# An own tile for the memory's transposed squares, and the other sequence's row squares transposed and summed in two steps

## The chip, the cores and the metric

The kernel runs on one core of a Trainium2 chip. The metric is the device time of one execution in microseconds (us), the median of several runs. Engines are named as the profile names them: PE (TensorE), DVE (VectorE), ACT (ScalarE), POOL (GpSimd) and SP (SyncE, which here only issues DMAs).

## The reference, cut to what matters

One encoder layer runs over two sequences of 512 tokens with 1024 channels each. In float32 it computes:

```
x = x + 0.5 * swiglu(rms_norm(x, ffn1_norm))                 # d_ff 2816
proj = rms_norm(x, mix_norm) @ w_in                          # q, k, v, memory q, k, v, gates
att  = attention(q, k, v)                                    # 8 heads of 64, 2 kv heads
mem  = sigmoid(o) * rms_norm_per_head(h_fwd + h_bwd)         # 4 memory heads of 128
x = x + (sigmoid(g_a) * (att @ w_up_att) + sigmoid(g_m) * (mem @ w_up_mlstm)) @ w_out
x = x + 0.5 * swiglu(rms_norm(x, ffn2_norm))
y = rms_norm(x, final_norm)
```

Two norms matter here. `rms_norm(x, ...)` needs, for each token, the sum of squares over 1024 channels. `rms_norm_per_head` needs, for each token and memory head, the sum of squares over 128 channels.

## The kernel before, in words

Activations lie with channels on the 128 partitions and the 512 tokens along the free axis. Every matrix product is made of three products of split values (high by high, high by low, low by high), each a 128x128 by 128x512 matmul on PE. So most tiles have a high part, which ACT writes by rounding, and a low part, which DVE writes by subtraction: both are in `split` (lines 725 to 728), the high part at L727 and the low part at L728.

The program has four stages: the first feed-forward network for both sequences, the mixing block of sequence 0 (generator `m0`), that of sequence 1 (`m1`), interleaved with the end of `m0`, and the second feed-forward network. A scheduler sets the order of instructions on each engine when the program is built, and it gives tiles their buffers out of pools in that order: a tile with the tag `f2` gets one of four buffers of 128x512 floats, a tile with the tag `R` one of two, and an instruction that writes a tile waits until the last reader of the tile that had the buffer before is done. Instructions wrapped in `pin` keep the order of the program text.

**Sums over partitions.** A sum of squares over channels is a sum over partitions. `block_sums` (L221 to L227) transposes the tile of squares in 32x32 blocks on DVE (L225) into a scratch tile with the tag `f2`, and reduces it to 128x16 on DVE (L226). `block_rstd` folds the four quarters with one small matmul on PE (L232) and takes the reciprocal root with twelve small DVE instructions (L235 to L241). `spread_rows` (L258) transposes the result back to 128x512.

**The other sequence's row squares in the attention.** While `m0` works through its eight attention heads (loop `for h in range(HA)`, `for b in range(4)`), it also makes the row norm of sequence 1, and `m1` makes the norm that sequence 0 needs for its second feed-forward network. These are passed in as `extra`: three functions `one`, `two` and `three` of `mid_parts` and `parts2`. They are called at b == 2 of heads 2, 3 and 4: `one` is `block_sums`, `two` is `block_rstd`, `three` is `spread_rows`. Beside them a head has DVE reduce each 128x512 score tile (L1115), take a reciprocal (L1118), scale some tiles (L1122), transpose probabilities in blocks (L1140), write low parts of probabilities (L728) and read the output bank (L1174); PE makes scores (L1112), values (L1159), transposes through the identity (L1128) and matmuls of the projection (L836) as filler in between.

**The memory heads of `m1`.** For each of four heads, `mem_head` makes the 512x512 weights, `mem_blocks` transposes them in 32x32 blocks on DVE (L1340), `mem_send` writes them to a DRAM buffer in eight DMAs on POOL's queue (L1348, `tbuf<-qt`), and `mem_out` reads them back in four pieces, each one DMA on POOL's queue (L1361, `f<-tbuf`) into a tile with the tag `f2`. Each piece is split (L727, L728), and PE multiplies it by the values: three matmuls a piece, `pso<-t,Vm` at L1374, two with the high part and one with the low. The DMAs of `mem_send` and `mem_out` and the L1374 matmuls are kept in program order among themselves; L850 matmuls (`mm<-att,w`, `mm<-xh,w`) fill PE in between. At the end of `mem_out` ACT copies and squares the sum (L1380, L1383), DVE multiplies the gate in (L1384), and then come `block_sums` into a tile `turned_` with the tag `f2`, `block_rstd`, `spread_rows` back into the same `turned_`, and its last reader at L1391. So `turned_` holds one of the four `f2` buffers from L225 to L1391, while the next head's pieces want four.

Among and after the last memory heads come eight units `mem_gate` (24 matmuls `mm<-xh,w` each, L850), most of them ahead of the fourth head's matmuls, and then the merge (L850, `pss<-mem,w`). In `m1` the first row blocks for the second network are prepared there: `prep2` loads a piece (L1808, `f<-x2buf`, tag `f2`, on SP), scales it (L723) and stores it (L1810, `xnbuf<-f`, on SP). SP also loads the weights (L293, `w<-wpark`).

Of the kernel before, what the change touches and what calls it, by code (L numbers as in the profile page):

```python
# [8 lines left out]
F32 = mybir.dt.float32  # L9
# [17 lines left out]
def encoder(ctx, tc, I, outs):  # L27
# [14 lines left out]
    def nm(s):  # L42
        n_id[0] += 1
        return f"{s}_{n_id[0]}"
# [15 lines left out]
    def T2(dtype=F32, tag="t2"):  # L60
        if tag in ("eb", "ac"):
            i = boxes[tag]
            boxes[tag] += 1
            return boxes["tile"][:, i % 4 + (4 if tag == "ac" else 0), :]
        if tag == "R":
            return spool.tile([P, S], dtype, tag="R", bufs=2, name=nm("R"))
        n = {"t2": 11, "f2": 4}[tag]
        return tpool.tile([P, S], dtype, tag=tag, bufs=n, name=nm(tag))
# [41 lines left out]
    def PO():  # L110
        return po_.tile([P, S], F32, tag="o", name=nm("pso"))
# [22 lines left out]
    def A(shape, dtype=F32, name="a"):  # L134
        return apool.tile(shape, dtype, tag="a", name=nm(name))
# [82 lines left out]
        nc.gpsimd.tensor_copy(fold[:, 32:P].rearrange("p (a j) -> p a j", j=32),  # L218
                              part_.unsqueeze(1).to_broadcast([P, 3, 32]))

    def block_sums(t, q=None):  # L221

        row = spool.tile([P, 64], F32, tag="row", bufs=1, name=nm("row"))
        q = T2(F32, "f2") if q is None else q
        nc.vector.transpose(q, t)  # L225
        nc.vector.tensor_reduce(row[:, 0:16], q.rearrange("p (n j) -> p n j", j=32), axis=AX.X, op=ALU.add)  # L226
        return row  # L227

# [630 lines left out]
    def mix(s, xh, xl, early=None, extra=None, after=None):  # L859
# [9 lines left out]
        def F2(dtype=F32):  # L869
            return T2(dtype, "f2")  # L870
# [136 lines left out]
        def gate_tops(run, top):  # L1007
            p = PT()
            pin(nc.tensor.transpose(p[:, 0:32], run, ident[0:32, 0:32]))
            pin(nc.tensor.transpose(p[:, 32:64], top.to_broadcast([32, P]), ident[0:32, 0:32]))  # L1010
            V_.tensor_copy(st[:, 0:2], p[:, 0:64].rearrange("p (i d b h) -> p i d b h", i=2, d=2, b=4))
# [44 lines left out]
        def q_rope(pr):  # L1056
            return rope_steps(qraw[:, :, pr * P:(pr + 1) * P], rq[0][:, :, 2 * pr:2 * pr + 2], tabs[0])

        def q_turn(pr, keep):
            p = pair_turn(qraw[:, :, pr * P:(pr + 1) * P], keep, MM if pr else PT)  # L1060
            for h, own, other in ((2 * pr, lower, upper), (2 * pr + 1, upper, lower)):
                nc.scalar.activation(qT[own, h, :], p[own, :], AF.Copy)
                V_.tensor_tensor(qT[other, h, :], p[own, :], f(qT[own, h, :]), op=ALU.subtract)
# [44 lines left out]
        def score(h, b):  # L1108
            hk = h // 4
            p = PS()  # L1110
            for j in range(2):
                pin(nc.tensor.matmul(p, qT[:, h, b * P:(b + 1) * P], kv[:, hk * 2 + j, :],  # L1112
                                     start=(j == 0), stop=(j == 1)))
            c = small(3, "asm")
            V_.tensor_reduce(c[:, 0:1], p, axis=AX.X, op=ALU.max, negate=True)  # L1115
            e = T2()
            nc.scalar.activation(e, p, AF.Exp, bias=c[:, 0:1], accum_out=c[:, 1:2])
            V_.reciprocal(c[:, 2:3], c[:, 1:2])  # L1118
            if b % 2 and (s or h or b < 3) or not s and h:
                nc.scalar.activation(e, e, AF.Copy, scale=c[:, 2:3])  # L1120
            else:
                V_.tensor_scalar(e, e, c[:, 2:3], None, op0=ALU.mult)  # L1122
            return e
# [15 lines left out]
        def turn_early(t, b):  # L1139
            V_.transpose(turned[:, :, b, :], t[:, 0:2 * P].rearrange("p (n m) -> p n m", m=32))  # L1140
# [63 lines left out]
        for h in range(HA):  # L1204
            nxt = []
            for b in range(4):
                if h in (0, 2, 4) and b == 2:
                    q_turn(h // 2 + 1, pin)
                if (h, b) == (0, 1):
                    gate_tops(*tops)  # L1210
                if (h, b) in ((0, 3), (2, 3)):
                    rope = q_rope(h // 2 + 2)
                if h < 4:
                    next(rope, None)
                if h + 1 < HA:
                    nxt.append(score(h + 1, b))
                if b in (3, 0) and h + b // 3 < (HA - 1 if not s else HA):
                    if b == 3:
                        for i in range(2):
                            turn_early(nxt[i], i)  # L1220
                    else:
                        for i in range(2, 4):
                            turn_early(Ps[i], i)
                if b == 1 and (h < HA - 1 or not (not s)):
                    send(h)
                n0, n1_ = FILLER if b else SOON
                among(n0)
                pp = None
                if b > 1:
                    pp = h, b, turn_keys(Ps, b)  # L1230
                elif h:
                    pp = h - 1, b, fetch(h - 1, b)
                among(n1_)
                if last:
                    values(*last)
                last = pp
                if extra and b == 2 and h in (2, 3, 4):
                    extra[h - 2]()
            Ps = nxt or Ps
        for b in range(2):  # L1240
            pp = HA - 1, b, turn_keys(Ps, b) if not s else fetch(HA - 1, b)
# [46 lines left out]
            return up_unit(1, d, mem, done, (PS, PT)[d % 2])  # L1288

        mem = A([P, HM, 2, S], F32R, "mem")  # L1290

        def mem_head(h):
            qk = qks[h]
# [58 lines left out]
        def mem_out(h, Ts):  # L1352
            moved = isinstance(Ts, int)
            vm = Vm[0]
            po = PO()
            hs_ = slice(h * P, (h + 1) * P)
            turned = []
            for j in range(4 + 1):
                if j < 4 and moved:
                    p = F2()  # L1360
                    mark(nc.gpsimd.dma_start(p, tbuf[Ts][4 * j:4 * j + 4].rearrange("c r a x -> (c r) (a x)")), True)  # L1361
                elif j < 4:
                    p = PT()
                    for i in range(4):
                        nc.tensor.transpose(p[:, i * P:(i + 1) * P], Ts[i][0][:, j * P:(j + 1) * P], ident)
                if j < 4:
                    ph, pl = T2(F32R), T2(F32R)
                    split(p, ph, pl)
                    turned.append((j, ph, pl))
                if j >= 1:  # L1370
                    t, ph, pl = turned.pop(0)
                    with shifted(15):
                        for n, (a, b) in enumerate(((0, ph), (1, ph), (0, pl))):
                            mark(nc.tensor.matmul(po, vm[:, a, t, hs_], b, start=(t == 0 and n == 0),  # L1374
                                                  stop=(t == 3 and n == 2)), True)
            h2 = T2()
            og = ogs[h]
            if moved:
                rows_ = T2()
                nc.scalar.activation(rows_.rearrange("p (i a m) -> p i a m", i=4, a=4),  # L1380
                                     po.rearrange("p (a i m) -> p i a m", i=4, a=4), AF.Copy)
                po = rows_
            nc.scalar.activation(h2, po, AF.Square)  # L1383
            V_.scalar_tensor_tensor(og, og, 1.0, po, op0=ALU.add, op1=ALU.mult)  # L1384
            turned_ = F2()
            row = block_sums(h2, turned_)
            with shifted(60):
                rh = block_rstd(row, DM)
            with shifted(160):
                Rh = spread_rows(rh, turned_)  # L1390
                V_.scalar_tensor_tensor(og, og, hn[:, h:h + 1], Rh, op0=ALU.mult, op1=ALU.mult)  # L1391
                split(og, mem[:, h, 0, :], mem[:, h, 1, :])

        if s:
# [3 lines left out]
            q = mem_blocks(0, mem_head(0))  # L1398
            at = [mem_send(*q)]
            go(*mem_values(), *qk2)  # L1400
            q = mem_blocks(1, mem_head(1))
# [3 lines left out]
            q = mem_blocks(2, mem_head(2))  # L1405
# [3 lines left out]
            q = mem_blocks(3, mem_head(3))  # L1409
# [338 lines left out]
    accs = [None, None]  # L1748
# [21 lines left out]
    R = [None, None]  # L1770
# [14 lines left out]
    def mid_parts(s):  # L1785
        got = []

        def one():
            got.append(block_sums(accs[s]))

        def two():
            got.append(block_rstd(got[0], D, pin))

        def three():
            R[s] = spread_rows(got[1], T2(F32, "R"))
        return one, two, three

    m0 = mix(0, *nhl[0], None, mid_parts(1), prep1)
    for _ in range(3):
# [1 line left out]
    acc2 = [None, None]  # L1801
# [14 lines left out]
    def parts2(s):  # L1816
        got = []

        def one():
            got.append(block_sums(acc2[s]))  # L1820

        def two():
            got.append(block_rstd(got[0], D, pin))

        def three():
            R2[s] = spread_rows(got[1], T2(F32, "R"))
        return one, two, three

    R2 = [None, None]
    m1 = mix(1, *nhl[1], None, parts2(0), prep2)  # L1830
# [152 lines left out]
```

## Time and profile before

| | us |
|---|---|
| median of 3 runs (lowest to highest) | 2033.63 (2033.22 to 2034.94) |
| the profiled execution | 2034.22 |
| its span, first to last instruction | 2032.4 |
| PE busy in the span | 2016.1 |
| DVE busy | 1593.8 |
| ACT busy | 919.9 |
| POOL busy | 253.4 |
| waits of PE for others, all together | 9.0 |

The profile is of one execution. A row of its timeline gives the start in us from the span's start, how long the rows merged in it took, engine, line, operation, output and inputs (buffer numbers left out), the shape, the count, and in brackets how long the engine had been idle before and what ended that. "f<-tbuf" is an instruction that writes a tile f from a tile tbuf. The waits of PE above are the sum of the rows "PE ... <- ..." of the table of waits (2.5, 1.6, 1.3, 1.0, 0.7, 0.7, 0.5, 0.3, 0.2 and 0.2). The matmul's ends in the profile are modelled; the starts are the better measure of PE's pace.

### The profile page before, as it was taken

The numbers are of one execution on the slowest core, as the hardware profiler recorded it, in microseconds if no ns is written. First come the engines' busy times: TensorE is split into PE (matmuls) and PEld (weight loads), VectorE is DVE, ScalarE is ACT, GpSimd is POOL, SyncE is SP. The second block draws the span as 40 slices with busy tenths as digits, with TensorE's granted clock in tenths as the row PEclk, the third lists the DMA queues.
The fourth block names the chain that finished last, engine by engine and source line by source line (L and its number), as shares of the span: only waits on it lengthen the run. The fifth ranks groups of instructions, "written<-read, shape, count | busy, mean of one in ns | idle before, by whom it ended". The sixth has DMA issues, their size and how long they took to land.

```text
span 2032.4 us, 26876 instructions
## 1 busy us (share of the span) xinstructions
PE 2016.1 (99%) x9129; PEld 1662.1 (82%) x9129; DVE 1593.8 (78%) x2830; ACT 919.9 (45%) x1677; POOL 253.4 (12%) x313
## 2 busy tenths in 40 slices
PE   9999999999999999999999999999999999999998
PEld 7888888888888887888888877888888888888887
DVE  7989999996698787886567867367798988786797
ACT  7644444443224477663325754145444444442224
POOL 0233333301003000100120022011000000000001
PEclk9999999999999999999999999999999999999999
DMA  9778786899766765868556677767565655699753
GB/s 312 232 234 266 237 276 229 276 346 363 270 218 225 266 195 184 282 212 293 194 188 209 195 246 259 252 204 242 159 208 169 227 166 180 204 334 348 270 199 120
DMA packets 329546, 482.11 MB, mean 237 GB/s; under 512 B 23016, under 2 KB 196160, under 8 KB 328128
## 3 DMA queue, kind: packets, MB, share of 16 engines
q1 hardware_dynamic: 316352, 439.27, 64.9%
q0 software_dynamic: 12896, 40.86, 5.8%
q8 instruction: 72, 1.18, 0.2%
q14 instruction: 66, 0.54, 0.1%
q10 hardware_dynamic: 160, 0.27, 0.0%
HBM read 308.70 MB, written 171.61 MB: 236 GB/s over the span
## 4 chain that ended last, share of the span: by engine, by line
PE 94%; DVE 2%; DMA 2%; ACT 1%; issue 0%; SPq 0%; DVEq 0%; ACTq 0%; POOLq 0%
PE mm L850 15%; PE pso L374 12%; PE pst L374 11%; PE mm L374 10%; PE mm L644 9%; PE pss L374 6%; PE mm L836 4%; PE pss L644 4%; PE pst L644 4%; PE mm L815 3%; PE pso L644 3%; PE pss L1112 1%; PE pso L1159 1%; PE pst L850 1%; PE pss L850 1%; PE pss L1302 1%
## 5 line engine op out<-in xcount | busy, mean ns | idle before, releaser
L374 PE MATMUL pst<-xc,w 128*128 128x512 f32 x1056 | 253.8, 389 | 1.0 <-ACT t L409 1.0
L374 PEld LDWEIGHTS pst<-xc,w 128*128 128x128 f32 x1056 | 198.2, 188 | 42.5 <-ACT t L409 1.4
L374 PE MATMUL mm<-xc,w 128*128 128x512 f32 x972 | 229.7, 390 | 0.3 <-ACT f L382 0.3
L374 PEld LDWEIGHTS mm<-xc,w 128*128 128x128 f32 x972 | 181.9, 188 | 38.6 <-ACT f L382 0.8
L644 PE MATMUL mm<-rt,w 128*128 128x512 f32 x765 | 178.7, 389 | 0.0
L850 PE MATMUL mm<-xh,w 128*128 128x512 f32 x560 | 176.3, 392 | 0.0
L644 PEld LDWEIGHTS mm<-rt,w 128*128 128x128 f32 x765 | 143.5, 188 | 29.7
L332 ACT ACTIVATE w<-t 128x512 fp32r<-128x512 f32 x176 | 107.5, 628 | 132.2 <-issue 63.1
L333 DVE TENSOR_TENSOR w<-t,w 128x512 fp32r<-128x512 f32 x176 | 120.8, 704 | 30.6 <-ACT w L332 28.9
L374 PE MATMUL pso<-xc,f 128*128 128x512 f32 x528 | 127.2, 390 | 0.1
L374 PE MATMUL pss<-xc,w 128*128 128x512 f32 x528 | 126.8, 389 | 0.0
L374 PE MATMUL pso<-xc,w 128*128 128x512 f32 x528 | 126.8, 389 | 0.0
L850 PEld LDWEIGHTS mm<-xh,w 128*128 128x128 f32 x560 | 105.2, 188 | 22.0
L374 PEld LDWEIGHTS pso<-xc,f 128*128 128x128 f32 x528 | 98.9, 188 | 21.5 <-DVE t L413 1.0
L374 PEld LDWEIGHTS pss<-xc,w 128*128 128x128 f32 x528 | 99.1, 188 | 20.6
L374 PEld LDWEIGHTS pso<-xc,w 128*128 128x128 f32 x528 | 99.1, 188 | 20.6
L836 PE MATMUL mm<-xh,w 128*128 128x512 f32 x336 | 110.4, 395 | 0.0
L850 PE MATMUL mm<-xl,w 128*128 128x512 f32 x280 | 109.7, 392 | 0.0
L727 ACT ACTIVATE w<-wr 128x512 fp32r<-128x512 f32 x72 | 45.1, 632 | 138.4 <-PE pso L644 70.6
L727 ACT ACTIVATE w<-t 128x512 fp32r<-128x512 f32 x82 | 51.8, 632 | 107.4 <-PE pst L644 62.4
L644 PE MATMUL pss<-rt,w 128*128 128x512 f32 x396 | 93.7, 389 | 0.0
L644 PE MATMUL pst<-rt,w 128*128 128x512 f32 x396 | 93.7, 389 | 0.0
(461 smaller groups left out, 4169.6 us busy)
## 6 DMA issues: line engine op xcount, KB each, us to landing
rt<-rbuf SPq DMA_DIRECT2D x154, 512.0 KB, 5.7
w<-wpark SPq DMA_DIRECT2D x112, 512.0 KB, 5.0
wpark<-w SPq DMA_DIRECT2D x64, 512.0 KB, 3.9
wr<-in_ffn_w_gate_dram SPq DMA_DIRECT2D x62, 512.0 KB, 5.5
wr<-in_ffn_w_up_dram SPq DMA_DIRECT2D x44, 512.0 KB, 4.7
rbuf<-f SPq DMA_DIRECT2D x86, 256.0 KB, 4.5
rbuf<-R SPq DMA_DIRECT2D x82, 256.0 KB, 4.7
rbuf<-tab SPq DMA_DIRECT2D x74, 256.0 KB, 4.1
```

The source lines that it names most:

```text
L332: pin(nc.scalar.activation(t[:, 0], src, AF.Copy))
L333: pin(V_.tensor_tensor(t[:, 1], src, f(t[:, 0]), op=ALU.subtract))
L374: nc.tensor.matmul(p, a[:, k, :], xt[:, b, k, :], start=(first and k == 0 and i == 0), stop=(k == HK_ - 1 and i == 2), skip_group_check=True)
L644: nc.tensor.matmul(p, u[:, a, d * P:(d + 1) * P], r[:, b, ts], start=(first and q == 0 and k == 0), stop=(q == len(us) - 1 and k == 2), sk ...
L727: nc.scalar.activation(hi, src, AF.Copy)
L815: mark(nc.tensor.matmul(p[b][:, :N], a[:, k, bs], w_[:, kl, :], start=(k == 0 and i == 0), stop=(k == KD - 1 and i == 2)), (kl, b, i) == ( ...
L836: pin(nc.tensor.matmul(p[0], a[:, k, :], b, start=(k == 0 and i == 0), stop=(k == n - 1 and i == 2)))
L850: mark(nc.tensor.matmul(p, a[:, k, :], b, start=(k == 0 and i == 0), stop=last), last)
L1112: pin(nc.tensor.matmul(p, qT[:, h, b * P:(b + 1) * P], kv[:, hk * 2 + j, :], start=(j == 0), stop=(j == 1)))
L1159: pin(nc.tensor.matmul(pos[h], Vst[:, kb, h // 4, :], w, start=(kb == KBS[0] and i == 0), stop=(kb == KBS[3] and i == 1)))
L1302: nc.tensor.matmul(p, qk[a][:, isl], qk[b], start=(n == 0), stop=(n == 2))
```

## The change

Three edits. The memory of `m1` gets one tile `own` with the tag `R`, made once, and all four heads use it as `turned_` in place of a new `f2` tile each. `block_sums` can stop after the transposition (`later=True`), and the new `block_adds` does the reduction. `one` becomes two functions, `one` and `one_`, and the schedule calls them at (h, b) = (2, 1) and (2, 2); `two` and `three` stay at (3, 2) and (4, 2).

```
-    def block_sums(t, q=None):
+    def block_sums(t, q=None, later=False):
         row = spool.tile([P, 64], F32, tag="row", bufs=1, name=nm("row"))
         q = T2(F32, "f2") if q is None else q
         nc.vector.transpose(q, t)
+        if later:
+            return row, q
+        return block_adds(row, q)
+
+    def block_adds(row, q):
         nc.vector.tensor_reduce(row[:, 0:16], q.rearrange("p (n j) -> p n j", j=32), axis=AX.X, op=ALU.add)
         return row
...
-                if extra and b == 2 and h in (2, 3, 4):
-                    extra[h - 2]()
+                if extra and (h, b) in ((2, 1), (2, 2), (3, 2), (4, 2)):
+                    extra[h - 2 + (h > 2 or b == 2)]()
...
         mem = A([P, HM, 2, S], F32R, "mem")
+        own = [T2(F32, "R")] if s else []
...
-            turned_ = F2()
+            turned_ = own[0] if own else F2()
             row = block_sums(h2, turned_)
...
         def one():
-            got.append(block_sums(accs[s]))
+            got.append(block_sums(accs[s], later=True))
+
+        def one_():
+            got[0] = block_adds(*got[0])
...
-        return one, two, three
+        return one, one_, two, three
```

`parts2` changes as `mid_parts` does, with `acc2` for `accs`. No instruction is added or taken away: PE, DVE, ACT, POOL and SP have as many as before. Buffers and the order are what differ. In the order of the changed program lines from L226 on have moved: L226 is L232 there, L232 is L238, L293 is L299, L728 is L734, L850 is L856, L1115 is L1121, L1118 is L1124, L1122 is L1128, L1140 is L1146, L1174 is L1180, L1374 is L1381, L1808 is L1818 and L1810 is L1820.

**PE, third memory head of `m1`.** These are the matmuls of its last two pieces (`pso`) among those of the attention's projection (`att`) and of the first `mem_gate` (`xh`, `xl`). Each piece has a high tile (x2) and a low one. Before:

```order
L1374 MATMUL pso_11385<-t_1457_11403,Vm_10719 128x512 x2
L850 MATMUL mm_11460<-att_9414,w_11354 128x512 x2
L1374 MATMUL pso_11385<-t_1458_11404,Vm_10719 128x512
L850 MATMUL mm_11477<-att_9414,w_11354 128x512 x3
L1374 MATMUL pso_11385<-t_1460_11412,Vm_10719 128x512 x2
L850 MATMUL mm_11477<-att_9414,w_11354 128x512 x3
L1374 MATMUL pso_11385<-t_1461_11413,Vm_10719 128x512
L850 MATMUL mm_11477<-att_9414,w_11354 128x512 x6
```

and in the changed program, up to the fold matmul of this head:

```order
L1381 MATMUL pso_11384<-t_1456_11402,Vm_10720 128x512 x2
L856 MATMUL mm_11458<-att_9414,w_11353 128x512 x2
L1381 MATMUL pso_11384<-t_1457_11403,Vm_10720 128x512
L1381 MATMUL pso_11384<-t_1459_11411,Vm_10720 128x512 x2
L1381 MATMUL pso_11384<-t_1460_11412,Vm_10720 128x512
L856 MATMUL mm_11475<-att_9414,w_11353 128x512 x12
L856 MATMUL mm_11492<-xh_8455,w_11455 128x512
L856 MATMUL mm_11492<-xl_8456,w_11455 128x512
L856 MATMUL mm_11492<-xh_8455,w_11455 128x512
L238 MATMUL pst_11429<-row_11426,fold 128x16
```

The last piece's three matmuls stand right behind the third piece's, ahead of the twelve that stood partly before them, and the fold matmul follows 15 matmuls after them (it was 15 before too, six of `att` and nine of the gate). POOL's order has not moved. What has is the buffer of the last piece: before, it takes over that of the first piece of the same head; now that of the last piece of the head before.

**DVE, attention of `m1`, head 2.** `R_9062` is the tile of squares. Before, the transposition and the sum stand among the work of b == 2:

```order
L1063 TENSOR_TENSOR qT_8643<-mm_9810,qT_8643 64x512
L728 TENSOR_TENSOR t_1169_9844<-pst_9838,t_1168_9843 128x512
L1174 TENSOR_TENSOR f_1138_9713<-pso_9751,f_1170_9852 64x512
L225 STREAM_TRANSPOSE f_1172_9858<-R_9062 128x512
L1115 TENSOR_REDUCE asm_9865<-pss_9862 128x1
L728 TENSOR_TENSOR att_9414<-f_1138_9713,att_9414 128x512
L226 TENSOR_REDUCE row_9857<-f_1172_9858 128x16
L1118 RECIPROCAL asm_9865<-asm_9865 128x1
L1140 STREAM_TRANSPOSE box_5409<-t_1151_9759 128x8x32
L1140 STREAM_TRANSPOSE box_5409<-t_1157_9786 128x8x32
L728 TENSOR_TENSOR t_1178_9884<-pst_9878,t_1177_9883 128x512
```

Now the transposition stands thirteen rows earlier and the sum fifteen, and at the old place other rows have closed up:

```order
L1121 TENSOR_REDUCE asm_9757<-pss_9754 128x1
L225 STREAM_TRANSPOSE f_1162_9811<-R_9062 128x512
L232 TENSOR_REDUCE row_9810<-f_1162_9811 128x16
L1124 RECIPROCAL asm_9757<-asm_9757 128x1
L1121 TENSOR_REDUCE asm_9784<-pss_9781 128x1
L1128 TENSOR_SCALAR t_1151_9759<-t_1151_9759,asm_9757 128x512
L734 TENSOR_TENSOR t_1154_9775<-f_1152_9772,t_1153_9774 128x512
```

Both instructions now delay the low part `t_1154`; before the low part `t_1178` there are now three of the block transpositions (`box`) and one score reduction more, in place of two block transpositions, the squares' transposition and their sum. In `m0` the pair has moved in the same way.

**SP, ahead of the merge of `m1`.** Pieces `x2buf` and `xnbuf` are those of `prep2`, `w<-wpark` are weights. Before:

```order
L293 DMA w_11707<-wpark_8371 128x1024 x2
L1808 DMA f_1518_11816<-x2buf_103 128x512
L1808 DMA f_1520_11839<-x2buf_103 128x512
L1808 DMA f_1523_11865<-x2buf_103 128x512
L293 DMA w_11737<-wpark_8407 128x1024 x2
L1810 DMA xnbuf<-f_1518_11816 128x512
```

and now:

```order
L299 DMA w_11704<-wpark_8371 128x1024 x2
L1818 DMA f_1515_11813<-x2buf_103 128x512
L1818 DMA f_1517_11836<-x2buf_103 128x512
L1818 DMA f_1520_11862<-x2buf_103 128x512
L1818 DMA f_1522_11885<-x2buf_103 128x512
L1820 DMA xnbuf<-f_1515_11813 128x512
L1820 DMA xnbuf<-f_1517_11836 128x512
L299 DMA w_11734<-wpark_8407 128x1024 x2
```

The fourth piece is loaded together with the first three, and two stores, which wait for DVE's scaling, stand ahead of a weight load.

More of the change, by code (lines that the diff above doesn't have):

```diff
@@ L1819, in one, with one_ @@
         def one():
-            got.append(block_sums(acc2[s]))
+            got.append(block_sums(acc2[s], later=True))
+        def one_():
+            got[0] = block_adds(*got[0])
         def two():
@@ L1826, in three @@
             R2[s] = spread_rows(got[1], T2(F32, "R"))
-        return one, two, three
+        return one, one_, two, three
     R2 = [None, None]
```

## The prediction

> **What bounds the kernel now.** I began with the page's first part, the busy time of each engine:
>
> ```profile
> PE 2016.1 (99%) x9129; PEld 1662.1 (82%) x9129; DVE 1593.8 (78%) x2830; ACT 919.9 (45%) x1677; POOL 253.4 (12%) x313
> ```
>
> PE works 2016.1 of the span's 2032.4 us, and the change leaves it the same 9129 matmuls. So only time in which PE waits, or runs slowly, can go or come. The profiled execution took 2034.22, of which 1.8 lie outside the span; the median is 2033.63. The table of waits comes next. Its columns are us in total, times, and the longest; these are the rows of PE in the places that the change touches:
>
> ```profile
> PE pso L1374 <- ACT t L727: 2.5, 1, 2.5
> PE pso L1159 <- DVE t L728: 0.7, 1, 0.7
> PE pso L1159 <- DVE f L1174: 0.2, 1, 0.2
> ```
>
> I then looked in the timeline for the wait of 2.5, in the third memory head of `m1`:
>
> ```profile
> 1266.61 0.45 PE L1374 MATMUL pso<-t,Vm 128*128 128x512 f32 x1
> 1266.89 0.86 PE L850 MATMUL mm<-att,w 128*128 128x512 f32 x3
> 1270.27 0.73 PE L1374 MATMUL pso<-t,Vm 128*128 128x512 f32 x2 [2.51 <-ACT t L727]
> ```
>
> and in the table of windows (us, PE busy and matmuls, granted clock, DMA share, GB/s) for a stretch ahead of it, the stretch that holds it, and the part right behind it:
>
> ```profile
> 1254.09:1262.02 7.93, 7.93 (x36) 1.00 0.61 186
> 1266.88:1276.78 9.90, 7.39 (x25) 0.83 0.79 253
> 1271.79:1275.17 3.38, 3.38 (x9) 0.51 0.64 199
> ```
>
> In each window one counted matmul was already running at its start, so 35, 24 and 8 start there. The first gives the pace: 7.93/35 = 0.227 us a matmul. At that pace the second window's 24 would take 5.44; they take 9.90, so 4.46 are lost. That is more than the wait. The three matmuls from 1266.89 on would be followed at 1266.89 + 3 x 0.227 = 1267.57; the next starts at 1270.27, 2.70 late. The third window loses 3.38 - 8 x 0.227 = 1.57, at a clock of 0.51. The rest, 0.19, lies at the edges. I count 1.57 for the clock and 2.89 for the wait with its edges.
>
> What ends late is the last of four pieces. POOL's rows, and the piece in the chain of waits:
>
> ```profile
> 1253.49 0.54 POOL L1361 DMA_DIRECT2D f<-tbuf  x1 [3.89 <-DVE row L239]
> 1264.57 0.54 POOL L1361 DMA_DIRECT2D f<-tbuf  x1 [10.53 <-DVE t L728]
> 1265.09 4.06 POOL L1348 DMA_DIRECT2D tbuf<-qt  x7
> 1263.37 0.67 DVE L728 TENSOR_TENSOR t<-f,t 128x512 fp32r<-128x512 f32 x1
> 1264.57 5.00 DMA f<-tbuf
> ```
>
> POOL issues the third fetch at 1253.49 and then stands still for 10.53 until DVE has written the low part of the same head's first piece (1263.37 + 0.67), since the fourth piece takes over that piece's buffer. The fetch lands 5.00 later, ACT rounds it, and PE goes on at 1270.27.
>
> **The own tile.** `turned_` no longer holds an `f2` buffer, so the four rotate among the pieces alone and the fourth piece takes that of the last piece of the head before, which was read long ago. Its fetch stands right behind the third on POOL, at 1253.49 + 0.54 = 1254.03. When is it ready?
>
> ```profile
> DMA to landing us min/median/max: 2.5/5.1/7.1
> 1259.54 1.14 ACT L727 ACTIVATE t<-f 128x512 fp32r<-128x512 f32 x2
> 1265.82 0.68 DVE L728 TENSOR_TENSOR t<-f,t 128x512 fp32r<-128x512 f32 x1
> 1273.38 0.71 DVE L225 STREAM_TRANSPOSE f<-t 128x512 f32<-128x512 f32 x1
> 1275.20 0.68 DVE L226 TENSOR_REDUCE row<-f 128x16 f32<-128x512 f32 x1
> ```
>
> By the median it lands at 1259.1, by the slowest fetch at 1261.1. ACT's two roundings at 1259.54 end at 1260.68 and a third is done by 1261.2 to 1261.8; PE wants it one matmul behind 1266.61, at 1266.84. The low part is DVE's next row behind 1265.82: it starts some 0.6 later and is written at about 1267.1. PE wants it three matmuls behind 1266.61 (the third piece's last, then two with the high part, then this one): 1266.61 + 3 x 0.227 = 1267.3. So 0.2 us are left; the cover is thin, and without it PE waits, which I bound at 0 to 0.4 (half a DVE instruction of 0.68). Behind it the fold matmul comes 15 matmuls (3.4) after the last `pso`. The chain to it is ACT's copy and square, L1384, L225 and L226. Before, the last `pso` started five matmuls behind 1270.27, at about 1271.5, L225 ended at 1274.1, and L226 came only at 1275.20 because a product for the gates (L1269) stood ahead of it; now that one stands behind L226. The chain is then 1274.1 + 0.68 - 1271.5 = 3.3 long, and the 15 matmuls and the `pso` itself give 16 x 0.227 = 3.6: 0.3 of cover, and 0 to 0.4 if it is gone. I take 0 for both, so this part gives back 4.46.
>
> POOL's eight sends `tbuf<-qt` of the fourth head no longer queue behind the fetch; they go 2 to 3 us earlier and nobody waits for them. The tile is shared by four heads, but DVE itself reads it last (L1391) ahead of the next L225, and no other `R` tile is taken in this stretch, so it costs nothing.
>
> A page speaks on the clock. The row: the 3.38 us window at 0.51 stands behind a wait of 2.51. The Trainium skill, "TensorE: Matmul & The Clock Gate", section "HAM oscillation — how this bites in real kernels", has the clock drop where PE idles for more than about 3.4 us. The trace disagrees on the length of the gap, 2.51 here, though the slow stretch is as long as the page's window. By the page's rule the gap would leave the clock whole and the gain of this part would be 2.89 instead of 4.46; that makes it a rival.
>
> **The attention of `m0`.** The transposition stood ahead of the read of the output bank, for which PE waits:
>
> ```profile
> 750.08 0.70 DVE L225 STREAM_TRANSPOSE f<-R 128x512 f32<-128x512 f32 x1
> 750.82 0.69 DVE L1174 TENSOR_TENSOR f<-pso,f 64x512 f32<-64x512 f32 x1
> 750.98 0.40 PE L836 MATMUL mm<-xh,w 128*128 128x512 f32 x1
> 751.56 0.73 PE L1159 MATMUL pso<-t,kv 128*128 128x512 f32 x2 [0.18 <-DVE f L1174]
> ```
>
> From 750.98 to 751.56 are 0.58 where 0.227 is the pace: 0.35 lost. Without the 0.70 ahead of it L1174 is done in time, and the 0.35 go. At the new place, one quarter of a head earlier, the pair delays tiles for which PE does not wait: 0.
>
> **The attention of `m1`.** Here PE waits for a low part behind the same pair:
>
> ```profile
> 1117.33 0.71 DVE L225 STREAM_TRANSPOSE f<-R 128x512 f32<-128x512 f32 x1
> 1118.08 0.69 DVE L1115 TENSOR_REDUCE asm<-pss 128x1 f32<-128x512 f32 x1
> 1119.29 0.68 DVE L226 TENSOR_REDUCE row<-f 128x16 f32<-128x512 f32 x1
> 1119.88 0.15 DVE L1118 RECIPROCAL asm<-asm 128x1 f32<-128x1 f32 x1
> 1119.95 0.75 DVE L1140 STREAM_TRANSPOSE box<-t 128x256 f32<-128x256 f32 x2
> 1120.63 0.65 DVE L728 TENSOR_TENSOR t<-pst,t 128x512 fp32r<-128x512 f32 x1
> 1120.26 0.42 PE L1159 MATMUL pso<-t,kv 128*128 128x512 f32 x1
> 1121.33 0.50 PE L1159 MATMUL pso<-t,kv 128*128 128x512 f32 x1 [0.65 <-DVE t L728]
> ```
>
> PE loses 1121.33 - 1120.26 - 0.227 = 0.84. L225 (to 1118.08: 0.75) and L226 (to 1119.88: 0.59) go from ahead of L728, together 1.34; by the order one more block transposition (0.75/2 = 0.38) and one more score reduction (0.60 apart from its neighbour) come in: 0.98. L728 is some 0.4 earlier, so 0.4 of the 0.84 go. The added reduction may have room of its own, hence up to 0.84; I take 0.4. At the new place:
>
> ```profile
> 1106.92 0.68 DVE L1115 TENSOR_REDUCE asm<-pss 128x1 f32<-128x512 f32 x1
> 1108.44 0.16 DVE L1118 RECIPROCAL asm<-asm 128x1 f32<-128x1 f32 x1 [0.85 <-ACT t L1117]
> 1109.04 0.68 DVE L728 TENSOR_TENSOR t<-f,t 128x512 fp32r<-128x512 f32 x1
> 1110.67 0.62 PE L1159 MATMUL pso<-t,kv 128*128 128x512 f32 x2
> ```
>
> the pair, 1.34, fills an idle 0.85 behind 1106.92, and L1118 and a score reduction (0.6) follow, so L728 ends near 1110.8 where it ended at 1109.7. PE wants it with the second matmul behind 1110.67, at 1110.9. The cover is 0.1; without it PE waits up to 0.2, and if all of the 1.34 pushed through, as much as 0.1 + 0.85. I take 0.
>
> **SP ahead of the merge.** A load of weights now stands behind two stores:
>
> ```profile
> 1305.34 0.80 SPq L293 DMA_DIRECT2D w<-wpark  x2
> 1306.23 1.38 SPq L1810 DMA_DIRECT2D xnbuf<-f  x3
> 1321.72 2.88 PE L850 MATMUL pss<-mem,w 128*128 128x512 f32 x12
> w<-wpark SPq DMA_DIRECT2D x28, 512.0 KB, 5.1
> ```
>
> Each store waits for DVE's scaling of its piece (L723), and then takes 0.46 to issue. Two move the load from 1305.34 to about 1307.2; it lands 5.1 later, at 1312.3. PE wants it at 1321.72, or 5 sooner now: 4 us of cover, cost 0. The fourth load `f<-x2buf`, moved forward with the first three, takes a buffer that is read at the same time as theirs.
>
> **The sum.** 4.46 + 0.35 + 0.4 = 5.2, and 2034.22 - 5.2 = 2029.0.
>
> **The rivals.** *The median holds no clock step.* The runs before lie between 2033.22 and 2034.94, a spread of 1.72, near the 1.57 of the step; the profiled one, which had it, stands 0.59 above the median. If the median run had none, the gain is 2.89 + 0.35 + 0.4 = 3.6, from 2033.63: 2030.0. For it speaks that spread; against it that the trace shows the step in the only execution seen. With no gain in the attention of `m1` and both thin covers lost it is 2033.63 - 2.89 - 0.35 + 0.8 = 2031.2.
>
> *The change does not do it.* If the fourth fetch still waited for a buffer on POOL, only the attentions gain, and lose as much at the new place: 2033.5. The order speaks against it.
>
> *Slower: the weights are late.* If the second store waited for its piece past 1316.3 (1321.72 less 5.1 and the issue), the merge would wait, us for us, and the clock step would come back behind that gap. At 1325, a wait of 9 and 1.57 for the clock against 5.2 gained: 2039. Against it: the stores before were out from 1306.23 on.
>
> **The numbers.** The forecast gets 0.60, the run without the step 0.26, no effect 0.08, the late weights 0.06. A measurement of this kernel can tell about 0.2%, 4.07 us, from no change: the line is 2029.56, right between the first two. Of the forecast's 0.60 I put 0.08 short of it (a thin cover lost), of the rival's 0.26 0.05 past it. Faster: 0.52 + 0.05 = 0.57; within: 0.08 + 0.21 + 0.08 = 0.37; slower 0.06. The range's low end takes the lowest run, 2033.22, less 4.46 + 0.35 + 0.84: 2027.6; its high end is the rival's 2031.2.
>
> **What would show it.** In the trace after: POOL's four fetches of the third head within 6 us, PE's wait at L1374 gone, no granted clock near 0.51 there, and L1159's wait of 0.7 at some 0.3. A wait at L1374 on DVE's low part, or one at the fold matmul, would be a thin cover lost. I am wrong if a wait of over 1 us stands anywhere in `m1` that was not there, or if PE lost its 4.46 for a reason that stays.

## The result and the profile after

| | before | after |
|---|---|---|
| median, us (lowest to highest) | 2034.76 (2031.63 to 2037.59), 16 runs | 2029.17 (2027.76 to 2033.28), 16 runs |
| ratio after to before | | 0.9975 (95% interval 0.9968 to 0.9982) |
| span of the profiled execution | 2032.4 | 2027.5 |

The change makes the kernel faster by 0.25%; 0.0025 x 2034.76 is 5.1 us, with an interval of 3.7 to 6.5. The two medians themselves lie 5.6 apart, within that interval. The forecast was 2029.0, with 5.2 us of gain, and the measured median is 2029.17.

First the table of waits of the kernel after, the four longest of PE's six rows (us in total, times, longest):

```profile
PE pss L1309 <- DVE t L1325: 1.7, 3, 0.7
PE pst L1468 <- DVE xc L1553: 1.6, 1, 1.6
PE mm L380 <- ACT t L388: 0.8, 2, 0.4
PE pst L380 <- ACT t L415: 0.5, 1, 0.5
```

The row for the memory head (2.5 before, now it would be L1381) is gone, and so are both rows for the attentions (now L1165). What is left does not touch the change.

The memory head: POOL, PE, ACT and DVE in the timeline after, then the window (us, PE busy and matmuls, granted clock, DMA share, GB/s). In the changed program the fetches stand in L1368 (L1361 before), the sends in L1355 (L1348) and the high parts in L733 (L727).

```profile
1253.89 1.06 POOL L1368 DMA_DIRECT2D f<-tbuf  x2 [4.07 <-DMA tbuf<-qt]
1262.24 4.64 POOL L1355 DMA_DIRECT2D tbuf<-qt  x8 [7.29 <-DVE qt L1347]
...
1259.54 1.66 ACT L733 ACTIVATE t<-f 128x512 fp32r<-128x512 f32 x3
...
1265.80 1.30 DVE L734 TENSOR_TENSOR t<-f,t 128x512 fp32r<-128x512 f32 x2
1269.89 0.69 DVE L232 TENSOR_REDUCE row<-R 128x16 f32<-128x512 f32 x1
...
1266.61 1.14 PE L1381 MATMUL pso<-t,Vm 128*128 128x512 f32 x4
1267.59 2.92 PE L856 MATMUL mm<-att,w 128*128 128x512 f32 x12
1271.03 0.29 PE L238 MATMUL pst<-row,fold 128*128 128x16 f32 x2
```

```profile
1266.88:1272.30 5.42, 5.42 (x26) 1.00 0.77 277
```

POOL issues the third and the fourth fetch together at 1253.89, where the fourth stood until 1264.57 before, and the eight sends start at 1262.24. ACT rounds three pieces in a row. DVE writes the last two low parts together, done at 1265.80 + 1.30 = 1267.10; PE takes the low one as the last of the four matmuls from 1266.61 on, near 1267.3. So the cover is the 0.2 that was forecast, and it held. The sum for the fold (DVE at 1269.89) ends at 1270.58, 0.45 ahead of the fold matmul at 1271.03. PE is busy through the whole window, at a clock of 1.00.

The attention of `m1`, DVE and PE after, at the new place of the pair and at its old one:

```profile
1108.08 0.70 DVE L225 STREAM_TRANSPOSE f<-R 128x512 f32<-128x512 f32 x1
1108.82 0.69 DVE L232 TENSOR_REDUCE row<-f 128x16 f32<-128x512 f32 x1
...
1110.62 0.69 DVE L734 TENSOR_TENSOR t<-f,t 128x512 fp32r<-128x512 f32 x1
...
1111.24 0.63 PE L1165 MATMUL pso<-t,kv 128*128 128x512 f32 x2
...
1115.79 0.45 DVE L1146 STREAM_TRANSPOSE box<-t 128x256 f32<-128x256 f32 x1
1116.26 0.69 DVE L734 TENSOR_TENSOR t<-pst,t 128x512 fp32r<-128x512 f32 x1
1116.98 0.69 DVE L1180 TENSOR_TENSOR f<-pso,f 64x512 f32<-64x512 f32 x1
...
1119.79 0.65 DVE L1121 TENSOR_REDUCE asm<-pss 128x1 f32<-128x512 f32 x1
1120.37 0.68 DVE L734 TENSOR_TENSOR t<-pst,t 128x512 fp32r<-128x512 f32 x1
...
1120.85 0.75 PE L1165 MATMUL pso<-t,kv 128*128 128x512 f32 x2
```

At the new place the low part is ready at 1111.31, and PE's second matmul behind 1111.24 wants it at 1111.47: a cover of 0.16, and no wait. At the old one the low part starts 0.48 ahead of PE's first matmul (1120.37 against 1120.85), where it started 0.37 behind it before (1120.63 against 1120.26). That is 0.85 earlier against PE, not 0.4, and PE does not wait: the low part is written at 1121.05, just ahead of PE's second matmul at 1121.10.

SP ahead of the merge, and the merge, after:

```profile
1299.72 1.58 SPq L1820 DMA_DIRECT2D xnbuf<-f  x2
1301.39 1.08 SPq L299 DMA_DIRECT2D w<-wpark  x2
...
1317.28 1.07 PE L856 MATMUL pss<-mem,w 128*128 128x512 f32 x4
```

The weight load does stand behind the two stores, and goes out at 1301.39; PE wants it 15.9 later. Before it was 1321.72 - 1305.34 = 16.4. So the move cost half a microsecond. Less the 5.1 that such a load took to land, some 10 us of cover are left. The forecast had 4: it moved PE's need forward by 5, but left SP's issues where they were.

**Where the 4.9 of the spans lie.** Both programs have 9129 matmuls. So the n-th matmul of one trace can be set against the n-th of the other, and the difference of their starts, stretch by stretch, says where time goes. The rows below are worked out so from the traces: each entry is what an execution gained within that stretch against the profiled execution of before (plus is faster), in us; the times in brackets are those of before. `own only`, `steps only` and `piece own` are experiments, told below; the four looks are the kernel before once more.

| | after | own only | steps only | piece own | look 1 | look 2 | look 3 | look 4 |
|---|---|---|---|---|---|---|---|---|
| first network (to 386) | -1.05 | -2.31 | -0.86 | -0.13 | 0.53 | -1.26 | -0.95 | -0.05 |
| attention of `m0` (749 to 755) | 0.35 | -0.01 | 0.35 | 0.00 | -0.01 | -0.01 | 0.00 | -0.01 |
| attention of `m1` (1114 to 1125) | 0.82 | 0.05 | 0.85 | 0.00 | -0.01 | -0.02 | 0.01 | -0.02 |
| third memory head (1262 to 1285) | 4.39 | 4.37 | 1.75 | 4.39 | 1.57 | -0.51 | -0.13 | 0.24 |

The three places of the change give 4.39 + 0.35 + 0.82 = 5.56 in the trace after. The spans differ by 4.9 because the first network, which the change does not touch, was 1.05 slower in that execution, and other untouched stretches gave some back. Such differences between executions lie between -2.3 and 0.5 in the first row, and they are why medians of this kernel need many runs.

### The profile page after: what moved, and what is told of

Read it like the earlier page. It is cut to its first block, busy times and chain, and to the rows that moved or that the text cites. A ratio compares the mean times of both kernels' runs of the same rounds, so it can differ in the third digit from the quotient of the medians.

```text
span 2027.5 us, 26874 instructions
## 1 busy us (share of the span) xinstructions
PE 2015.1 (99%) x9129; PEld 1661.4 (82%) x9129; DVE 1592.6 (79%) x2830; ACT 919.2 (45%) x1677; POOL 249.7 (12%) x313
## 4 chain that ended last, share of the span: by engine, by line
PE 94%; DVE 2%; DMA 2%; issue 1%; ACT 1%; SPq 0%; DVEq 0%; ACTq 0%
PE mm L856 16%; PE mm L380 11%; PE pso L380 11%; PE pst L380 11%; PE mm L650 9%; PE mm L842 5%; PE pss L380 5%; PE pss L650 4%; PE pst L650 4%; PE mm L821 3%; PE pso L650 3%; PE pss L1118 1%; PE pso L1165 1%; PE pso L1381 1%; PE pst L856 1%; PE pss L856 1%
## 5 line engine op out<-in xcount | busy, mean ns | idle before, releaser
L856 PE MATMUL mm<-xh,w 128*128 128x512 f32 x560 | 176.0, 391 | 0.0
L856 PEld LDWEIGHTS mm<-xh,w 128*128 128x128 f32 x560 | 104.9, 188 | 21.8
L856 PE MATMUL mm<-xl,w 128*128 128x512 f32 x280 | 109.6, 391 | 0.0
L733 ACT ACTIVATE w<-wr 128x512 fp32r<-128x512 f32 x72 | 45.1, 632 | 138.3 <-PE pso L650 70.6
L733 ACT ACTIVATE w<-t 128x512 fp32r<-128x512 f32 x82 | 51.8, 632 | 107.4 <-PE pst L650 62.4
```

Of the source, the lines that this page charges most:

```text
L733: nc.scalar.activation(hi, src, AF.Copy)
L856: mark(nc.tensor.matmul(p, a[:, k, :], b, start=(k == 0 and i == 0), stop=last), last)
```

## The experiments

The theory: the fourth fetch waited on POOL for the first piece's buffer, and that wait, with what it does to the clock, is most of the gain; the attentions give some 1 us. The rivals: the gain is the attentions'; or the clock step does not belong to the wait.

**Own tile only** (`own_only`): the two lines with `own`, nothing else.

```
+        own = [T2(F32, "R")] if s else []
...
-            turned_ = F2()
+            turned_ = own[0] if own else F2()
```

Expected: 

> Only the own tile; the squares' transposition and sum of the attentions stay together where they were. By the prediction this is the memory head's term alone: 4.46 us less than before (2.89 of the wait and 1.57 of the clock), and the two waits of PE at L1159 (0.7 and 0.2) stay. If the clock step does not belong to this wait, 2.9 less. If the gain came from the attentions, nothing.

Measured: ratio 0.9982 (0.9973 to 0.9991), that is 3.7 us (1.8 to 5.5). The times allow 4.46 as well as 2.9. In the trace the memory head gives 4.37 and the attentions nothing; PE's waits there, 0.7 and 0.2 before, stand:

```profile
PE pso L1159 <- DVE t L728: 0.6, 1, 0.6
PE pso L1159 <- DVE f L1174: 0.2, 1, 0.2
```

So the memory head's gain is the own tile's alone.

**The two steps only** (`steps_only`): all but these two lines.

```
-        own = [T2(F32, "R")] if s else []
...
-            turned_ = own[0] if own else F2()
+            turned_ = F2()
```

Here the diff is against the changed kernel. Expected: 

> Only the two steps in the attentions; the heads' tile is taken from the four f2 buffers as before. By the prediction 0.35 + 0.4 = 0.75 us less than before, by the trace after 0.3 + 0.8 = 1.1; the wait of 2.5 at L1374 and a clock near 0.5 behind it stay. In the times this is hardly above what they can tell. If the gain of the whole change came from here: 4 to 5 less.

Measured: ratio 0.9999 (0.9990 to 1.0008), a gain of 0.2 us with an interval from 2.0 gained to 1.6 lost: the times cannot tell 1.1 from nothing, but they exclude 4 to 5. The trace has 0.35 and 0.85 at the attentions, as after. It also has a surprise, in PE's timeline and the windows:

```profile
1271.69 0.73 PE L1380 MATMUL pso<-t,Vm 128*128 128x512 f32 x2 [2.18 <-ACT t L733]
```

```profile
1267.19:1270.61 3.42, 2.33 (x10) 1.00 1.02 401
1270.61:1274.02 3.41, 2.33 (x10) 1.00 0.73 239
1274.02:1277.43 3.41, 3.41 (x17) 1.00 0.77 214
```

The wait stays, as expected, but the clock does not fall behind it. That part of the expectation failed, and it is most of why this execution lost 1.75 less in the memory head than the profiled one of before; the rest, 0.34, is a shorter wait.

**A tile for the fourth piece** (`piece_own`): before, with the `R` tile for another user.

```
+        own = [T2(F32, "R")] if s else []
...
-                    p = F2()
+                    p = own[0] if j == 3 else F2()
```

Expected: 

> The kernel before, with one R tile for the fourth piece of every head in place of one for the turned squares, which keep an f2 buffer; no two steps. If what counts is that the fourth fetch need not wait for the first piece of its own head, this gains what the own tile gains: 4.4 less than before, no wait at L1374. If it counts that the turned squares leave the f2 buffers, the wait stays and the time is that of before.

Measured: ratio 0.9980 (0.9972 to 0.9989), 4.1 us (2.2 to 5.7), and 4.39 in the memory head. POOL's rows:

```profile
1254.90 0.54 POOL L1362 DMA_DIRECT2D f<-tbuf  x1 [4.07 <-DVE mg L1269]
1255.43 0.54 POOL L1362 DMA_DIRECT2D R<-tbuf  x1
```

The fourth fetch (into `R`) goes right behind the third, though the turned squares still take an `f2` buffer. So what counts is one buffer more in the rotation, not who leaves it.

**The gap filled with work** (`fill12`): before, with twelve more matmuls ahead of the fourth piece's.

```
+                        if s and h == 2 and t == 3:
+                            for _ in range(12):
+                                mark(nc.tensor.matmul(po, vm[:, 0, 2, hs_], third[0], start=False, stop=False), True)
+                        third = [ph]
```

Expected: 

> The kernel before with twelve extra matmuls right ahead of the fourth piece's three in the third memory head of m1 (they repeat a product of the third piece, so the sum of that head is another one). The fetch stays late. They cost 12 x 0.227 = 2.72 us of work and stand where PE waited 2.70; about 0.9 of waiting is left, since three matmuls of the projection move behind. If the idle time made the clock drop, the 1.57 go and the sum is 2.72 - 2.70 - 1.57 - 0.19 + 0.87 = 0.9 less than before; if the clock drops there for another reason, 0.7 more than before, and a stretch near 0.5 stands in the trace.

Measured: ratio 1.0000 (0.9992 to 1.0009), which holds both 0.9 less and 0.7 more; the times decide nothing. The timeline of POOL and PE, and the window behind:

```profile
1267.72 0.54 POOL L1361 DMA_DIRECT2D f<-tbuf  x1 [9.90 <-DVE t L728]
...
1270.05 2.89 PE L1375 MATMUL pso<-t,Vm 128*128 128x512 f32 x12
1273.12 1.23 PE L1378 MATMUL pso<-t,Vm 128*128 128x512 f32 x3 [0.18 <-ACT t L727]
```

```profile
1273.00:1276.40 3.40, 3.28 (x13) 1.00 0.59 168
```

The fetch is as late as before, PE works through the twelve and waits 0.18, and the clock stays at 1.00. Over the memory head this execution is 0.97 ahead of before with twelve matmuls (2.72) more. That is the expected 0.9 of the theory. With the step missing in `steps_only` too, one trace without it proves little, so the next runs took the kernel before itself.

**The kernel before, four more profiled executions** (`look1` to `look4`), unchanged. Expected of the first: 

> The kernel before, unchanged, one of four more profiled executions. All four hold the wait of about 2.5 at L1374. If the clock is set in fixed stretches of 3.413 us (the lengths in the profile's clock record) and drops for one of them only where a stretch was idle for about half or more, the step of 1.57 stands behind the wait in some executions and not in others: there where one stretch holds 1.9 or more of the wait, not where two share it. If the drop belongs to the wait by its length alone, all four show it.

Of the others: 

> The second of the four, with the same expectation: step or no step by how the wait of 2.5 lies across the stretches of 3.413 us.

> The third of the four, with the same expectation: step or no step by how the wait of 2.5 lies across the stretches of 3.413 us.

> The fourth of the four, with the same expectation: step or no step by how the wait of 2.5 lies across the stretches of 3.413 us.

Measured, single executions: 2032.56, 2037.44, 2036.29 and 2035.43, on another chip than the experiments above. PE's first two matmuls of the fourth piece, look 1 to look 4:

```profile
1270.84 0.73 PE L1374 MATMUL pso<-t,Vm 128*128 128x512 f32 x2 [2.36 <-ACT t L727]
1273.62 0.73 PE L1374 MATMUL pso<-t,Vm 128*128 128x512 f32 x2 [3.04 <-ACT t L727]
1273.10 0.74 PE L1374 MATMUL pso<-t,Vm 128*128 128x512 f32 x2 [2.66 <-ACT t L727]
1272.00 0.74 PE L1374 MATMUL pso<-t,Vm 128*128 128x512 f32 x2 [2.26 <-ACT t L727]
```

The clock is granted in stretches of 3.413 us: in the profiled execution of before, the clock is at 1.0 from 8.78 for 1262.93 us, which is 370 x 3.4133, then at 0.5 for one such stretch. So the edges of the stretches can be counted on from there, and the windows cut along them. For each execution the stretch that held most of the wait, and the one behind it; the second column is PE's busy time. Before:

```profile
1268.30:1271.71 3.41, 1.44 (x6) 1.00 0.88 298
1271.71:1275.12 3.41, 3.41 (x9) 0.50 0.63 196
```

look 1:

```profile
1266.87:1270.28 3.41, 1.61 (x7) 1.00 1.03 400
1270.28:1273.70 3.42, 2.86 (x12) 1.00 0.66 183
```

look 2, look 3 and look 4:

```profile
1271.03:1274.44 3.41, 0.82 (x4) 1.00 0.80 272
1274.44:1277.86 3.42, 3.42 (x10) 0.50 0.55 169
```

```profile
1270.55:1273.97 3.42, 0.87 (x4) 1.00 0.96 352
1273.97:1277.39 3.42, 3.42 (x10) 0.50 0.58 182
```

```profile
1269.88:1273.30 3.42, 1.30 (x6) 1.00 0.96 336
1273.30:1276.71 3.41, 3.41 (x10) 0.50 0.63 175
```

Where PE was busy 1.44 or less of a stretch, the next one ran at half clock; at 1.61 (look 1) and 2.33 (`steps_only`, whose wait lies across an edge) it did not. All ten traces of this case, cut the same way, hold 14 stretches with PE busy for 1.44 us or less, these four and ten at the kernel's end, and each was followed by half clock; no stretch with 1.61 or more was. Both figures rest on modelled ends of matmuls, and where between them the limit lies is open. The length of the wait alone does not order the executions: the fourth piece came 2.34 late in `steps_only` and 2.53 in look 1, without the step, and 2.43 late in look 4, with it.

The Trainium skill, "TensorE: Matmul & The Clock Gate", section "What's actually happening", has a free-running window of 3413 ns, and the traces agree with that length and with its being free-running: the clock first rises at 8.78 us in before and at 7.35, 4.69, 11.04 and 6.96 in the looks, which are not whole stretches apart. Its table there has the clock fall after an idle window; here no stretch was idle altogether, and a PE busy for 1.44 of 3.41 was enough.

What the memory head loses against after follows from the table of gains: 4.39 in before, and 4.39 less the row's entry elsewhere. How late the fourth piece came is the start of its first matmul less that of the one ahead, less the pace of 0.227.

| us | lost | fourth piece late | lost beyond that | PE busy in the stretch | clock of the next |
|---|---|---|---|---|---|
| before | 4.39 | 2.68 | 1.71 | 1.44 | 0.50 |
| look 1 | 2.82 | 2.53 | 0.29 | 1.61 | 1.00 |
| look 2 | 4.90 | 3.21 | 1.69 | 0.82 | 0.50 |
| look 3 | 4.52 | 2.82 | 1.70 | 0.87 | 0.50 |
| look 4 | 4.15 | 2.43 | 1.72 | 1.30 | 0.50 |
| `steps_only` | 2.64 | 2.34 | 0.30 | 2.33 | 1.00 |

So the step costs 1.4 us, when it comes, and it came in four of six executions.

## Why the prediction was right

**The memory head.** Right by each step: the buffer that POOL waited for, the fetch behind the third, the ready times (1267.10 against a forecast of 1267.1), the fold in time. The term was 4.46 and the trace has 4.39, against the execution from which the term was read.

**The clock.** The forecast took the 1.57 of one execution as part of every run. That term is mis-sized: it is worth 1.4, and came in four of six executions. By these traces the rival that the median holds none was wrong as well; the truth is between. The mean loss of the six in the memory head is (4.39 + 2.82 + 4.90 + 4.52 + 4.15 + 2.64) / 6 = 3.90. The timed runs only hint at two kinds: of 33 runs of before, 17 had a mean granted clock of 0.998 and 16 one of 0.999, and their medians were 2034.55 and 2033.43; of the 16 after none was under 0.999. The mean clock also holds the start and the end of a run, so it does not count steps: look 4 had one and reads 0.999, and two of the 11 runs of `own_only`, in whose trace the wait is gone, read 0.998.

**The attentions.** In `m0` 0.35 was forecast and 0.35 found, in two traces. In `m1` 0.4 was forecast and 0.82 and 0.85 found, all of PE's wait. What failed is the count by which one more block transposition and one more score reduction, 0.98 together, come in where the pair's 1.34 goes. Between the read of the output bank and the low part only the reduction came in. The added transposition stands ahead of the low part at 1116.26 (row 1115.79), outside the stretch that was counted. The read of the output bank before:

```profile
1116.61 0.69 DVE L1174 TENSOR_TENSOR f<-pso,f 64x512 f32<-64x512 f32 x1
```

From the read of the output bank to the low part it is 1120.37 - 1116.98 = 3.39 after and 1120.63 - 1116.61 = 4.02 before: 0.63 less, not 0.4. And that read itself came 0.22 earlier against PE's matmul (3.87 ahead of it, 3.65 before). The 0.84 was named as the upper end.

**The sum.** With the sizes found it would be 3.90 + 0.35 + 0.83 = 5.1, which is the measured 5.1. The times alone could not tell: with the step in no run the memory head would give 2.7 (the mean of look 1 and `steps_only`) and the sum 3.9, with it in every run 4.5 and 5.7, and both lie within 3.7 to 6.5. So how often the step comes rests on the six traces. The forecast of 5.2 held because the 0.56 that the memory head gives less and the 0.43 that the attention gives more nearly cancel, which is luck. It is luck too that 2029.0 lies within 0.2 us of the median: it was counted from one execution of 2034.22, and the median before is 2034.76.

**The other rivals.** The fetch did go, so the change did what it says. The slower case, a late weight load on SP, had some 10 us of cover. Neither thin cover was lost: no wait of PE stands at either place. That a longer DVE queue at these places would break them was not tried.

## What to carry to other kernels

When a wait's releaser is an engine that read a buffer, count the users of the buffer's pool: here three pieces and a short-lived helper left the fourth piece waiting on its own head, and one more buffer, given to either user, removed the wait. Price such a wait in several executions: besides its length it may cost a clock step or not, by where it falls. And compare two traces matmul by matmul at the places of the change, since executions differ by 2 us elsewhere.

## What the runs showed that was not expected

- The granted clock is set in stretches of 3.413 us that do not start with the kernel. A stretch in which PE was busy 1.44 us or less was followed by one at half clock; with 1.61 or more it was not.
- A wait of 2.3 to 3.2 us cost 0.3 or 1.7 us beyond its length, by how much of it fell into one stretch, so one kernel with such a wait had executions 1.4 us apart for that reason alone.
- One transfer moved a run by 1.4 us at an untouched place. In `steps_only` PE's score matmul L1308 at 1202.87 came 2.15 late, in before the same one 0.75 late. DVE, for which it waits, had stood still for the second of two loads; in before DVE took that one up without a wait. Why the load came later is open. The row of `steps_only`, then that of before:

```profile
1199.51 0.69 DVE L1091 TENSOR_TENSOR box<-box,tab 128x512 f32<-128x512 f32 x1 [1.42 <-DMA box<-ebuf]
...
1197.64 0.69 DVE L1085 TENSOR_TENSOR box<-box,tab 128x512 f32<-128x512 f32 x1
```
